# Small transfers of a decoder kernel issued from GpSimd's queue instead of SyncE's

## The chip, the cores and the metric

The kernel runs on one core of a Trainium2 chip. A core has TensorE (PE, matrix products), VectorE (DVE), ScalarE (ACT), GpSimd (POOL) and SyncE (SP). Each works through its own instructions in order, and semaphores tie them together. A DMA is issued by an instruction on one of these engines' queues, here SP's in the kernel before, and carried out by 16 DMA engines beside the others. The metric is the time of one execution on the device in microseconds.

## The reference

The kernel computes a trunk of two layers over 512 tokens of 1024 channels, in float32. Layer 0 mixes tokens by sliding-window attention, layer 1 by a gated delta rule; each is followed by a feed-forward product with a short convolution in its gate.

```
x += swa_sink_attention(rms_norm(x))        # 16 heads of 64, window of 128
x += (silu(causal_dwconv(gate) + b) * up) @ w_down
x += gated_deltanet(rms_norm(x))            # 8 key heads, 16 value heads of 128
x += (silu(causal_dwconv(gate) + b) * up) @ w_down
...
gc = cumsum(g);  decay = exp(gc_c - gc_s) below the diagonal
kk = k k^T;  a = 1 + strict_lower(beta * kk * decay)
u, w = solve(a, [v * beta, k * beta * exp(gc)])
v_new = u - w S;  o = q exp(gc) S + (q k^T * decay) v_new
S = S * exp(gc_last) + (k exp(gc_last - gc))^T v_new
```

The delta rule is a recurrence over blocks of tokens; within a block its triangular system `a` has to be inverted.

## The kernel before, in words

Activations are kept channel-major, 128 channels by 512 tokens in a tile. Every dense product runs over weight tiles of 128 by 1024 that the method `weight` (L125) loads to `raw` and splits in a high part `whi` (ACT, L134) and a low part `wlo` (DVE, L135); PE then makes three products per slice of 128 (L145 to L147), 24 matmuls for a tile. `raw`, `whi` and `wlo` have three buffers each, so that a new tile is loaded when the tile three back has been split.

The work that is not dense (attention, gates, decays, solve, recurrence) is written as generators. `pump` (L93) takes one step of whichever is due between two grains of the dense products. So the order of the instructions on every engine is fixed when the program is built; a scheduler of the framework then sets it and adds the semaphore waits. A DMA waits, besides its producers, for the one that used the same semaphore lane, eight DMAs earlier on its issuer's kind of queue (the names DMAHW0 to DMAHW7 and DMASW0 to DMASW7 in the orders below).

In the gated-delta layer much data takes a way through DRAM because its layout has to change between partitions:
- `decays` (L769) goes over eight head pairs `hk`. Rows of cumulated decays are broadcast to all partitions (`D<-rowd`, L796, two loads per pair); DVE subtracts and masks (L807), ACT takes the exponential (L809), and the result is stored (`Dd<-D`, L810). DVE then multiplies it into the products of keys (L815), and that goes to DRAM too (`kkd<-kd`, L817).
- `solve` (L822) reads the 32 by 32 triangles of all heads, with other partitions, in four loads (`X<-kkd`, L836), inverts them on DVE (L838 to L845), and stores them straight (`Td<-X`, L851, four) and transposed (`Nd<-t`, L859, six).
- `prologue` (L885) of each head pair loads `kk`, `D`, `kt` and `qd` (L897 to L900), then pieces of the inverses `NT` (L908, three) and `TT` (L911, four), and joins them to inverses of 128 rows by matmuls on PE (L920 on `NT`, L931 on `TT` and what follows). Two tiles are first set to zero by POOL (L895, L896). `vb` is loaded at L966 and `z` in `epilogue` at L1018. The values, `z` and the keys are stored at L694, L730 and L674.
- `run` (L1047) loads x and the constants, stores the residual `hd` (L1076) and writes the output (L1072); `h` comes back at L745.

All of this goes through `self.aux`, which is SP's queue (L79), or is written with `nc.sync` itself. SP issues the weights in the same queue, in program order.

Of the kernel before, what the change touches and what calls it, by code (L numbers as in the profile page):

```python
# [17 lines left out]
P = 128  # L18
# [6 lines left out]

# ---------------------------------------------------------------- host layout
def layout(x, positions, mixer_norm, ffn_norm, attn_w_in, attn_q_gain, attn_k_gain, attn_sinks,
           attn_w_out, gdn_w_in, gdn_conv, gdn_a_log, gdn_dt_bias, gdn_norm, gdn_w_out,
           ffn_w_up, ffn_conv, ffn_conv_b, ffn_w_down):
    """Arrays of the launch: the inputs in other orders, and constants of the shapes alone."""  # L30
    c = np.ascontiguousarray
    a = {}
    a["xT"] = c(x[0].T.reshape(KT, P, T))
    a["up"] = c(ffn_w_up.reshape(2, KT, P, 2, 24, P).transpose(0, 4, 3, 2, 1, 5)).reshape(2, 24, 2, P, 1024)
    a["down"] = c(ffn_w_down.reshape(2, 3, 8, P, 8, P).transpose(0, 1, 4, 3, 2, 5)).reshape(2, 3, 8, P, 1024)
    cols = []
    cols.append(mixer_norm.reshape(2, KT, P).transpose(2, 0, 1).reshape(P, 16))
    cols.append(ffn_norm.reshape(2, KT, P).transpose(2, 0, 1).reshape(P, 16))
    cols.append(ffn_conv.reshape(2, 3, 24, P).transpose(3, 0, 2, 1).reshape(P, 144))
    cols.append(gdn_conv[0].reshape(4, 32, P).transpose(2, 1, 0).reshape(P, 128))  # L40
    cols.append(gdn_norm[0].reshape(P, 1))
    cols.append(ffn_conv_b.reshape(2, 24, P).transpose(2, 0, 1).reshape(P, 48))
    w = attn_w_in[0]
    w = np.concatenate([w[:, 1024:1280], w[:, :512], w[:, 1280:], w[:, 512:1024]], axis=1)
    a["win"] = c(w.reshape(2, 4, P, 6, 256).transpose(3, 0, 2, 1, 4)).reshape(6, 2, P, 1024)
    wo = attn_w_out[0].reshape(2, 2, 4, 64, D).transpose(0, 2, 1, 3, 4).reshape(KT, P, KT, P)
    a["wout"] = c(wo.reshape(2, 4, P, KT, P).transpose(0, 3, 2, 1, 4)).reshape(2, KT, P, 512)
    a["rows"] = c(np.concatenate([attn_q_gain[0], attn_k_gain[0], attn_sinks[0]]))
    a["pos"] = c(positions[0].reshape(NB, P).T)
    a["freq"] = (500000.0 ** (-np.arange(0, 16, 2, dtype=np.float64) / 16)).astype(np.float32)  # L50
    i, j = np.arange(P)[:, None], np.arange(2 * P)[None]
    a["band"] = np.where((i + P - j >= 0) & (i + P - j < P), 0.0, -1e30).astype(np.float32)
    a["cols"] = c(np.concatenate(cols, axis=1))
    w = gdn_w_in[0].reshape(KT, P, -1).transpose(1, 0, 2)
    a["gin"] = c(w[:, :, :6144].reshape(P, KT, 48, P).transpose(2, 0, 1, 3)).reshape(48, P, 1024)
    a["gba"] = c(w[:, :, 6144:]).reshape(P, KT * 32)
    a["gout"] = c(gdn_w_out[0].reshape(2, 8, P, KT, P).transpose(0, 3, 2, 1, 4)).reshape(2, KT, P, 1024)
    a["grow"] = c(np.concatenate([gdn_a_log[0], gdn_dt_bias[0]]))
    a["tri"] = c(np.triu(np.ones((P, P), np.float32)))
    a["low"] = np.where(np.arange(P)[None] < np.arange(P)[:, None], -1e30, 0.0).astype(np.float32)  # L60
    a["ident"] = np.eye(P, dtype=np.float32)
    return a
# [5 lines left out]
class Builder:  # L68
    def __init__(self, tc, ctx, ins, out):
        self.tc, self.nc, self.ins, self.out = tc, tc.nc, ins, out  # L70
        pool = lambda name, bufs, **kw: ctx.enter_context(tc.tile_pool(name=name, bufs=bufs, **kw))
        self.const = pool("const", 1)
        self.wp = pool("wp", 3)
        self.big = pool("big", 36)
        self.tmp = pool("tmp", 8)
        self.small = pool("small", 3)
        self.gx = pool("gx", 1)
        self.ps = pool("ps", 8, space=bass.MemoryType.PSUM)
        self.aux = tc.nc.sync  # L79
        self.queue, self.now, self.seq = [], 0, 0  # L80
        self.dram = pool("dram", 1, space=bass.MemoryType.DRAM)
        nc = self.nc
        self.cols = self.const.tile([P, C_END], F32, name="cols")
        self.ident = self.const.tile([P, P], F32, name="ident")
        self.ones = self.const.tile([P, 1], F32, name="ones")
        nc.vector.memset(self.ones, 1.0)

    # ---- tasks that are traced between the grains of the dense products
    def spawn(self, gen, delay=0):
# [20 lines left out]

    # ---- allocation
    def psum(self):
# [10 lines left out]

    # ---- float32 operands as sums of two parts that one pass carries
    def weight(self, src, cols=1024, parts=1):  # L125
# [29 lines left out]

    # ---- 1/sqrt of a small tile, in place of x
    def rsqrt(self, y, x, n):
# [9 lines left out]

    # ---- rms norm: the operand (gain * h) in two parts, and 1/rms of each token
    def norm_tile(self, h, m, gain):
# [43 lines left out]
    def normalise(self, h, m, gain):  # L213
        """the operand again, with 1/rms in it"""
        nc = self.nc
# [7 lines left out]

    # ---- feed-forward
    def ffn(self, l, h, after):
# [32 lines left out]

    # ---- sine and cosine of the rotary angles, token-major
    def rope(self):  # L260
        nc = self.nc
# [3 lines left out]
        pos = self.ax.tile([P, NB], I32, name="pos", bufs=1)  # L265
        nc.sync.dma_start(pos, self.ins["pos"])
        fr = self.ax.tile([P, 8], F32, name="fr", bufs=1)
        nc.sync.dma_start(fr, self.ins["freq"].partition_broadcast(P))
        pf = self.ax.tile([P, NB], F32, name="pf", bufs=1)
# [62 lines left out]

    # ---- sliding-window attention
    def attn_setup(self):
        nc = self.nc
        rows = self.ax.tile([P, 144], F32, name="rows", bufs=1)
        nc.sync.dma_start(rows, self.ins["rows"].partition_broadcast(P))
        self.rows = rows
        self.gcol = self.ax.tile([P, 2], F32, name="gcol", bufs=1)
        nc.vector.memset(self.gcol, 1.0)  # L340
        for i in range(2):
            for j in range(2):
                nc.sync.dma_start(self.gcol[j * 64 + 16:j * 64 + 64, i:i + 1], self.ins["rows"][i * 64 + 16:i * 64 + 64].unsqueeze(1))
        nc.vector.tensor_scalar(self.gcol[:, 0:1], self.gcol[:, 0:1], 0.125, None, op0=ALU.mult)
        self.band = self.ax.tile([P, 2 * P], F32, name="band", bufs=1)
        nc.sync.dma_start(self.band, self.ins["band"])
        self.rope()

    def qk_norm(self, pss, dst, gain):
        """dst [P, 2, 8, 64], by pairs of blocks and (block, head) <- rotary(rms_norm(rstd * pss)),  # L350
        without the gain of the dims past the rotary ones"""
        nc = self.nc
# [188 lines left out]

    # ---- gated delta rule
    def in_tile(self, j, u):
# [5 lines left out]
    def conv(self, j, ps, dst, raw=False):  # L549
        """dst <- silu(causal conv of channels of tile j), channel-major"""  # L550
        nc = self.nc
# [10 lines left out]
    def turn(self, src):  # L562
        """[128, (4, 128)] psum <- four transposed blocks"""
        pt = self.psum()
# [8 lines left out]
    def gates(self, u, ready):  # L573
        """decays and beta of (token, block, head); gc and its exponential by rows too"""
        nc, gx = self.nc, self.gx
# [74 lines left out]
    def gdn(self, h, hd, stack, after):  # L650
# [87 lines left out]
        for half in range(2):  # L738
# [4 lines left out]
            for m in range(KT):  # L743
                if half == 0:
                    nc.sync.dma_start(hp[m], hd[m])  # L745
                hi, lo = self.weight(self.ins["gout"][half, m])
# [22 lines left out]
    def decays(self, sp, ready):  # L769
        """of each head: decay between two tokens of a block, and the strictly lower systems (rows by s)"""  # L770
        nc = self.nc
# [50 lines left out]
    def solve(self, sp, ready):  # L822
        """inverses of the 32-row triangles, two of each partition's (half, head, block)"""
        nc = self.nc
# [60 lines left out]
    def prologue(self, rx, hk, ready):  # L885
# [27 lines left out]
        jn = [(j, n) for j in range(2) for n in range(NB)]  # L913
        # 32 -> 64 rows
        px = self.psum()
# [21 lines left out]
        while "rq" not in ready:  # L937
            yield 1
        # products of queries and keys
        qk = self.psum()  # L940
# [6 lines left out]
        yield 2  # L947
        # 64 -> 128 rows
        px = self.psum()
# [97 lines left out]
    def run(self, stages):  # L1047
# [5 lines left out]
        for m in range(KT):  # L1053
            nc.sync.dma_start(h[m], self.ins["xT"][m])
            if m == 0:
                nc.sync.dma_start(self.cols, self.ins["cols"])
            if self.first and m in (0, 1):
# [3 lines left out]
            else:  # L1061
                self.norm_tile(h[m], m, gains[stages[0]])
        nc.sync.dma_start(self.ident, self.ins["ident"])
        if self.first:
# [3 lines left out]
        for i, s in enumerate(stages):  # L1068
# [4 lines left out]
            if s == "gdn":  # L1073
                hd = self.dram.tile([KT, P, T], F32, name="hd")
                for m in range(KT):
                    nc.sync.dma_start(hd[m], h[m])  # L1076
                h = self.gdn(h, hd, stack, after)
# [24 lines left out]
```

## Time and profile before

| | us |
|---|---|
| median of 3 runs | 1584.66 |
| fastest, slowest run | 1578.55, 1584.74 |
| span of the profiled execution | 1579.8 |
| PE busy | 1502.6 (95%) |
| DVE busy | 903.3 (57%) |
| ACT busy | 677.0 (43%) |
| POOL busy | 10.4 (1%) |

No time of the profiled execution is recorded beside its span; the span lies between the fastest run and the median. Busy times of engines overlap. The share of PE is a mean over the whole: the dense stages run at full PE and the gated-delta layer, roughly 640 to 1120 us, less so. A wait names the engine that stood still, the line it stood at, and what ended the wait. The landing of a DMA is the time from its issue on a queue to the end of its transfer.

### The profile page before, as it was taken

The numbers are of one execution on the slowest core, as the hardware profiler recorded it, in microseconds if no ns is written. First come the engines' busy times: TensorE is split into PE (matmuls) and PEld (weight loads), VectorE is DVE, ScalarE is ACT, GpSimd is POOL, SyncE is SP. The second block draws the span as 40 slices with busy tenths as digits, with TensorE's granted clock in tenths as the row PEclk, the third lists the DMA queues.
The fourth block names the chain that finished last, engine by engine and source line by source line (L and its number), as shares of the span: only waits on it lengthen the run. The fifth ranks groups of instructions, "written<-read, shape, count | busy, mean of one in ns | idle before, by whom it ended". The sixth has DMA issues, their size and how long they took to land. (4 is left out here: it accounts for less than half of the span.)

```text
span 1579.8 us, 20924 instructions
## 1 busy us (share of the span) xinstructions
PE 1502.6 (95%) x7914; PEld 1232.7 (78%) x7914; DVE 903.3 (57%) x1818; ACT 677.0 (43%) x1515; POOL 10.4 (1%) x21
## 2 busy tenths in 40 slices
PE   7999999999999999977888999989999999999998
PEld 7965688888888888766676887777788888888887
DVE  7675666445535658744478655555566644644652
ACT  6586643223323345534325456543453323322331
POOL 0000000000000000000000000000000000000000
PEclk9999999999999999998899999989999999999999
DMA  5201232332232243355685645544122232223222
GB/s 178 66 26 29 81 107 94 99 102 94 93 100 100 94 140 111 131 164 178 192 231 116 204 152 164 149 136 129 55 93 94 93 107 94 93 99 101 95 100 73
DMA packets 104572, 179.96 MB, mean 114 GB/s; under 512 B 45336, under 2 KB 57624, under 8 KB 104472
## 3 DMA queue, kind: packets, MB, share of 16 engines
q1 hardware_dynamic: 104472, 178.63, 35.8%
q8 instruction: 62, 1.02, 0.3%
q14 instruction: 38, 0.31, 0.1%
HBM read 153.60 MB, written 25.00 MB: 113 GB/s over the span
## 5 line engine op out<-in xcount | busy, mean ns | idle before, releaser
L147 PE MATMUL ps<-a,wlo 128*128 128x512 f32 x1736 | 685.7, 395 | 27.0 <-DVE wlo L135 27.0
L145 PE MATMUL ps<-a,whi 128*128 128x512 f32 x1736 | 695.0, 401 | 5.7 <-ACT whi L134 4.5
L146 PE MATMUL ps<-a,whi 128*128 128x512 f32 x1736 | 684.4, 394 | 0.0
L134 ACT CAST whi<-raw 128x1024 fp32r<-128x1024 f32 (+1 forms) x239 | 242.2, 1015 | 466.3 <-PE ps L146 394.5
L147 PEld LDWEIGHTS ps<-a,wlo 128*128 128x128 f32 x1736 | 329.6, 190 | 100.5 <-DVE wlo L135 30.2
L145 PEld LDWEIGHTS ps<-a,whi 128*128 128x128 f32 x1736 | 330.2, 190 | 79.9 <-ACT whi L134 5.4
L146 PEld LDWEIGHTS ps<-a,whi 128*128 128x128 f32 x1736 | 330.0, 190 | 66.8 <-DVE a L141 0.8
L135 DVE TENSOR_TENSOR wlo<-raw,whi 128x1024 fp32r<-128x1024 f32 (+1 forms) x239 | 280.3, 1174 | 61.7 <-ACT whi L134 58.3
L255 DVE TENSOR_TENSOR h<-h,ps 128x512 f32<-128x512 f32 x48 | 33.0, 688 | 148.5 <-PE ps L147 148.5
L240 DVE TENSOR_TENSOR t<-ps,rbc 128x512 f32<-128x512 f32 x48 | 33.2, 691 | 106.2 <-PE ps L147 106.1
L246 DVE TENSOR_TENSOR t<-ps,rbc 128x512 f32<-128x512 f32 x48 | 33.2, 692 | 90.8 <-PE ps L147 90.8
L244 ACT ACTIVATE t<-t 128x512 f32<-128x512 f32 x48 | 30.4, 632 | 97.7 <-DVE t L243 97.7
L145 PE MATMUL ps<-whi,a 128*128 128x256 f32 x192 | 57.2, 299 | 8.7 <-ACT a L189 8.7
L146 PE MATMUL ps<-wlo,a 128*128 128x256 f32 x192 | 55.5, 289 | 0.5 <-DVE wlo L135 0.5
L147 PE MATMUL ps<-whi,a 128*128 128x256 f32 x192 | 55.5, 289 | 0.0
L807 DVE SCALAR_TENSOR_TENSOR D<-D,both,low 128x128 f32<-128x128 f32 x64 | 18.1, 347 | 57.8 <-DMA D<-rowd 57.8
L145 PEld LDWEIGHTS ps<-whi,a 128*128 128x128 f32 x192 | 37.8, 197 | 10.7 <-ACT a L189 8.7
L559 DVE SCALAR_TENSOR_TENSOR t<-ps,cols,t 128x511 f32<-128x511 f32 (+2 forms) x48 | 35.6, 745 | 17.4 <-ACT t L557 10.9
L140 ACT CAST a<-t 128x512 fp32r<-128x512 f32 x48 | 30.0, 624 | 33.3 <-DVE t L247 33.3
L241 ACT ACTIVATE t<-t,cols 128x512 f32<-128x512 f32 x48 | 38.9, 811 | 2.0 <-DVE t L240 2.0
L146 PEld LDWEIGHTS ps<-wlo,a 128*128 128x128 f32 x192 | 37.9, 197 | 0.7 <-DVE wlo L135 0.7
L147 PEld LDWEIGHTS ps<-whi,a 128*128 128x128 f32 x192 | 37.8, 197 | 0.1
(245 smaller groups left out, 1431.3 us busy)
## 6 DMA issues: line engine op xcount, KB each, us to landing
raw<-in_up SPq DMA_DIRECT2D x96, 512.0 KB, 3.6
raw<-in_down SPq DMA_DIRECT2D x48, 512.0 KB, 3.6
raw<-in_gin SPq DMA_DIRECT2D x48, 512.0 KB, 4.7
raw<-in_gout SPq DMA_DIRECT2D x16, 512.0 KB, 3.7
raw<-in_win SPq DMA_DIRECT2D x10, 512.0 KB, 4.0
raw<-in_wout SPq DMA_DIRECT2D x16, 256.0 KB, 2.6
zd<-t SPq DMA_DIRECT2D x16, 256.0 KB, 4.8
D<-rowd SPq DMA_DIRECT2D x16, 256.0 KB, 12.7
```

Of the source, the lines that this page charges most:

```text
L134: nc.scalar.copy(hi[:, s], raw[:, s])
L135: nc.vector.tensor_tensor(lo[:, s], raw[:, s], hi[:, s].bitcast(F32), op=ALU.subtract)
L140: nc.scalar.copy(hi, src)
L145: mm(ps, w[0], x[0], start=first, stop=False)
L146: mm(ps, w[0], x[1], start=False, stop=False)
L147: mm(ps, w[1], x[0], start=False, stop=last)
L240: nc.vector.tensor_tensor(g, gu[0], self.bc, op=ALU.mult)
L241: nc.scalar.activation(y, g, AF.Identity, bias=self.col(C_FB + l * 24 + j), scale=self.col(cw + 2))
L244: nc.scalar.activation(y, y, AF.Silu)
L246: nc.vector.tensor_tensor(t, gu[1], self.bc, op=ALU.mult)
L255: nc.vector.tensor_tensor(h[m], h[m], ps, op=ALU.add)
L559: nc.vector.scalar_tensor_tensor(dst[:, i:], g[:, :T - i], self.col(cw + 3 - i), dst[:, i:], op0=ALU.mult, op1=ALU.add)
```

## The change

`self.aux` becomes GpSimd's queue, and the transfers that named SP's queue, except the weights (L133), the x tiles (L1054) and the output (L1072), go through `self.aux` too. Comments and some docstrings also go; no line number changes. The computation, the tiles and their buffers are the same.

```
-        self.aux = tc.nc.sync
+        self.aux = tc.nc.gpsimd
...
-        nc.sync.dma_start(pos, self.ins["pos"])
+        self.aux.dma_start(pos, self.ins["pos"])
...
-        nc.sync.dma_start(fr, self.ins["freq"].partition_broadcast(P))
+        self.aux.dma_start(fr, self.ins["freq"].partition_broadcast(P))
...
-        nc.sync.dma_start(rows, self.ins["rows"].partition_broadcast(P))
+        self.aux.dma_start(rows, self.ins["rows"].partition_broadcast(P))
...
-                nc.sync.dma_start(self.gcol[j * 64 + 16:j * 64 + 64, i:i + 1], self.ins["rows"][i * 64 + 16:i * 64 + 64].unsqueeze(1))
+                self.aux.dma_start(self.gcol[j * 64 + 16:j * 64 + 64, i:i + 1], self.ins["rows"][i * 64 + 16:i * 64 + 64].unsqueeze(1))
...
-        nc.sync.dma_start(self.band, self.ins["band"])
+        self.aux.dma_start(self.band, self.ins["band"])
...
-                    nc.sync.dma_start(hp[m], hd[m])
+                    self.aux.dma_start(hp[m], hd[m])
...
-                nc.sync.dma_start(self.cols, self.ins["cols"])
+                self.aux.dma_start(self.cols, self.ins["cols"])
...
-        nc.sync.dma_start(self.ident, self.ins["ident"])
+        self.aux.dma_start(self.ident, self.ins["ident"])
...
-                    nc.sync.dma_start(hd[m], h[m])
+                    self.aux.dma_start(hd[m], h[m])
```

In the order of instructions SP goes from 479 DMAs to 255, and POOL from none to 224. PE's order stays nearly the same. Three places show it. The first is SP's queue in the kernel before, at the decays of the first head pairs (D are the decay rows, Dd and kkd their stores in DRAM, zd a store of z, raw a weight tile):

```order
167 L133 DMA raw<-in_gin 128x1024 [waits DVE_49]
168 L810 DMA Dd<-D 128x1024 [waits DMAHW2_49,DMAHW1_49,Activation_49]
169 L817 DMA kkd<-kd 128x1024 [waits DVE_49]
170 L730 DMA zd<-t_5912 128x512 [waits DMAHW3_49,Activation_49]
171 L810 DMA Dd<-D 128x1024 [waits DMAHW4_49,Activation_49]
172 L796 DMA D<-rowd 128x4x128 [waits DMAHW5_49,DMAHW1_49]
173 L796 DMA D<-rowd 128x4x128 [waits DMAHW6_49]
174 L730 DMA zd<-t_5964 128x512 [waits DMAHW7_49,Activation_49]
175 L817 DMA kkd<-kd 128x1024 [waits DMAHW0_49,DVE_49]
176 L796 DMA D<-rowd 128x4x128 [waits DMAHW4_49]
177 L796 DMA D<-rowd 128x4x128 [waits DMAHW2_49]
```

The same place on POOL's queue in the kernel after:

```order
44 L810 DMA Dd<-D 128x1024 [waits DMASW1_49,DMASW0_49,Activation_49]
45 L817 DMA kkd<-kd 128x1024 [waits DVE_49]
46 L730 DMA zd<-t_5912 128x512 [waits DMASW2_49,Activation_49]
47 L796 DMA D<-rowd 128x4x128 [waits DMASW0_49]
48 L796 DMA D<-rowd 128x4x128
49 L810 DMA Dd<-D 128x1024 [waits DMASW5_49,Activation_49]
50 L730 DMA zd<-t_5964 128x512 [waits DMASW6_49,Activation_49]
51 L817 DMA kkd<-kd 128x1024 [waits DMASW7_49,DVE_49]
52 L796 DMA D<-rowd 128x4x128 [waits DMASW5_49]
53 L796 DMA D<-rowd 128x4x128 [waits DMASW1_49]
```

The weight loads that stood between the bounces are on SP's queue, where each waits for its buffer and its lane only. The bounces stand in nearly the same order among themselves; here the third pair's two D loads come ahead of the second pair's store Dd (row 49), where before that store stood ahead of them (row 171).

The second place is the end of the solve, on POOL in the kernel after (Nd and Td are the stores of the inverses, NT and TT the loads of the first head pair):

```order
100 L847 MEMSET X 128x2x32 [waits DVE_49]
101 L859 DMA Nd<-t_6895 64x16x32 [waits DMASW6_49,Activation_49]
102 L851 DMA Td<-X 64x32x32 [waits DMASW7_49,DVE_49,Pool_49]
103 L851 DMA Td<-X 64x32x32 [waits DMASW0_49]
104 L851 DMA Td<-X 64x32x32 [waits DMASW1_49]
105 L851 DMA Td<-X 64x32x32 [waits DMASW2_49]
106 L859 DMA Nd<-t_6895 64x16x32 [waits DMASW3_49]
107 L859 DMA Nd<-t_6899 64x16x32 [waits DMASW4_49,Activation_49]
108 L859 DMA Nd<-t_6899 64x16x32 [waits DMASW5_49]
109 L859 DMA Nd<-t_6903 64x16x32 [waits DMASW6_49,Activation_49]
110 L859 DMA Nd<-t_6906 64x16x32 [waits DMASW7_49,Activation_49]
111 L908 DMA NT<-Nd 32x8x32 [waits DMASW4_49,DMASW0_49]
```

On SP in the kernel before these DMAs stood in the same order, behind five weight loads in a row. They have all moved to POOL, where a MEMSET of X (L847) stands ahead of them.

The third place is the start, on DVE in the kernel after (a are the normalised inputs, h the x tiles, cols the gains):

```order
4 L344 TENSOR_SCALAR gcol<-gcol 128x1 [waits DMASW4_49,DMASW3_49,DVE_49]
5 L190 SCALAR_TENSOR_TENSOR a_105<-h_85,cols,a_104 128x512 [waits DMAHW0_49,DMASW0_49,Activation_49]
6 L135 TENSOR_TENSOR wlo<-raw,whi 128x512 [waits DMAHW1_49,Activation_49]
7 L135 TENSOR_TENSOR wlo<-raw,whi 128x512 [waits DMAHW2_49,Activation_49]
8 L190 SCALAR_TENSOR_TENSOR a_119<-h_86,cols,a_118 128x512 [waits DMAHW3_49,Activation_49]
9 L135 TENSOR_TENSOR wlo<-raw,whi 128x512 [waits DMAHW4_49,Activation_49]
10 L135 TENSOR_TENSOR wlo<-raw,whi 128x512 [waits DMAHW5_49,Activation_49]
11 L270 CAST pf<-pos 128x4 [waits DMASW0_49]
```

In the kernel before the first of these is a wlo of L135, and gcol (L344) and pos (L270) come behind all the L190. Now L344 stands ahead of them and waits for the loads of gcol on POOL's queue, and the first L190 waits for cols there.

## Rows read from the trace of the kernel before

**Rows 1.** The page: the span, and section 1, busy time by engine.
```profile
span 1579.8 us, 20924 instructions
...
PE 1502.6 (95%) x7914; PEld 1232.7 (78%) x7914; DVE 903.3 (57%) x1818; ACT 677.0 (43%) x1515; POOL 10.4 (1%) x21
...
```

**Rows 2.** Busy time by stretch; columns in the header row.
```profile
...
core 0: us, PE busy (x) PEld busy (x) DVE busy (x) ACT busy (x) POOL busy (x), PEclk, DMA share, GB/s
...
240.00:280.00 40.00, 40.00 (x179) 33.10 (x178) 23.19 (x29) 15.40 (x19) 0.00 (x0) 1.00 0.30 104
...
669.00:782.00 113.00, 85.76 (x360) 68.51 (x358) 50.58 (x119) 40.52 (x69) 1.19 (x2) 0.86 0.52 171
...
853.00:880.00 27.00, 20.90 (x169) 16.23 (x168) 17.10 (x37) 17.81 (x56) 0.00 (x0) 0.87 0.66 125
...
```

**Rows 3.** Waits of PE, 669 to 890 us: who waited for whom, total, times, longest.
```profile
...
PE ps L147 <- DVE wlo L135: 27.0, 7, 10.0
PE ps L567 <- ACT t L560: 6.0, 1, 6.0
...
```

**Rows 4.** Waits of DVE, 669 to 890 us.
```profile
...
DVE D L807 <- DMA D<-rowd: 57.8, 13, 11.7
...
DVE X L838 <- DMA X<-kkd: 2.4, 1, 2.4
...
```

**Rows 5.** The page, section 6: issues of D<-rowd, KB each, us to landing.
```profile
...
D<-rowd SPq DMA_DIRECT2D x16, 256.0 KB, 12.7
```

**Rows 6.** Waits of SP's DMA queue, 669 to 782 us.
```profile
...
SPq L133 <- DVE wlo L135: 17.3, 4, 6.9
SPq L817 <- DVE kd L815: 10.9, 6, 3.2
SPq L796 <- DMA Dd<-D: 8.5, 3, 5.7
SPq L810 <- DMA D<-rowd: 8.1, 2, 4.0
SPq L810 <- ACT D L809: 6.4, 3, 2.3
...
```

**Rows 7.** Line 133's weight loads, 669 to 782 us: landing.
```profile
...
DMA to landing us min/median/max: 6.7/14.0/16.5
```

**Rows 8.** Line 133's weight loads, 240 to 600 us: landing.
```profile
...
DMA to landing us min/median/max: 3.5/3.6/4.6
```

**Rows 9.** Line 851's issues: min/median/max ns of one.
```profile
...
L851 SPq DMA_DIRECT2D Td<-X x4: 635/1794/2417, 853.5 to 857.8; - x4
...
```

**Rows 10.** Line 911's loads TT<-Td: landing.
```profile
...
DMA to landing us min/median/max: 2.2/6.5/7.8
```

**Rows 11.** Line 836's loads X<-kkd: issue in ns, and landing.
```profile
...
L836 SPq DMA_DIRECT2D X<-kkd x4: 648/1696/2778, 783.8 to 788.7; - x4
...
DMA to landing us min/median/max: 6.0/6.1/6.3
```

**Rows 12.** Timeline of SP's queue, 850 to 882 us: start, length.
```profile
...
852.76 0.60 SPq L859 DMA_DIRECT2D Nd<-t  x1
853.46 6.78 SPq L851 DMA_DIRECT2D Td<-X  x4
...
865.57 1.58 SPq L908 DMA_DIRECT2D NT<-Nd  x2
...
```

**Rows 13.** Timeline of PE, 852 to 880 us.
```profile
...
871.43 0.24 PE L920 MATMUL ps<-NT,kk 32*32 32x32 f32 x2
...
874.49 0.22 PE L931 MATMUL ps<-TT,x 32*32 32x32 f32 x2
...
```

**Rows 14.** Timeline of SP's queue, 930 to 970 us: two kk loads.
```profile
...
934.95 0.32 SPq L897 DMA_DIRECT2D kk<-kkd  x1
...
968.16 0.32 SPq L897 DMA_DIRECT2D kk<-kkd  x1
...
```

**Rows 15.** Timeline of PE, 0 to 12 us: the first matmul.
```profile
...
8.68 0.58 PE L145 MATMUL ps<-whi,a 128*128 128x256 f32 x1 [8.68 <-ACT a L189]
...
```

## Prediction

> **What bounds the kernel now.** I read the page's shares first, then the busy time by stage, then the waits of PE, DVE and SP in the stages where PE is not full, then the landings of the DMAs that end those waits. PE is busy for 1502.6 of 1579.8 us [rows 1], so only 77 us can be won without less work on PE, while a stall of PE adds its full length. Outside the gated-delta layer PE has nothing to gain: from 240 to 280 us it is busy for 40.00 of 40 us [rows 2]. The same row gives the pace of dense work: 179 matmuls in 40 us are 0.223 us each, and a weight tile of 24 matmuls lasts 5.4 us. The idle time lies where small transfers through DRAM share SP's queue with the weights. From 669 to 782 us (the decays of eight head pairs) PE is idle for 27.2 us and its granted clock is 0.86; from 853 to 880 us (end of the solve) it is idle for 6.1 us [rows 2]. In the first stretch PE's wait is for wlo, the low half of a weight, 27.0 us in 7 waits up to the start of the recurrence [rows 3]. But DVE, which makes wlo, stands behind L807, the decay rows D<-rowd, for 57.8 us in 13 waits [rows 4]; one such load takes 12.7 us to land [rows 5]. A weight is late there because DVE is held in order behind a bounce through DRAM.
>
> **What the change removes: the weights leave that queue.** 224 of SP's 479 DMAs go to POOL; SP keeps weights, x and output. Between 669 and 782 us SP held its queue for 17.3 us for a weight buffer, and for 10.9 + 8.5 + 8.1 + 6.4 = 33.9 us for the bounce traffic's own producers [rows 6]. The first part no longer stands ahead of a bounce; the second goes to POOL with the bounces, whose order there is nearly the old one (the third pair's D loads gain one place on a store, which I leave out). Bounds: 0, if the transfers themselves are the limit, and -27.0 us, all of PE's wait. I take the weights' share of the holding: 27.0 x 17.3 / 51.2 = 9.1, so **-9 us**. The reverse shows as well: a weight takes 14.0 us to land in this stage [rows 7] against 3.6 in the feed-forward [rows 8], because it stands behind the broadcasts. That is worth nothing by itself, since PE's wait is DVE's wait for D, not for raw.
>
> The landing of 14.0 against 3.6 us says that much of the delay is inside the transfers and not at the issue [rows 7, 8]. The Trainium skill (DMA: Bandwidth & Descriptors, section "Issuing engines are not separate DMA queues") states that DMAs started by the scalar, sync or gpsimd engine run on the same 16 engines and interleave, and that starting them from several engines saves only the time to initiate them. By that rule the term would be nearer 0 than -9 and the forecast 9 us later.
>
> **What it adds: the price of a piece on POOL.** No DMA of before is issued by POOL, so its price is unknown; its trace has 21 POOL instructions [rows 1]. I count pieces, the runs of contiguous bytes that a transfer's shape has: 2048 in each Td<-X (64x32x32) and X<-kkd, 1024 in each Nd<-t, 256 in each NT and TT load (32x8x32), 512 in each D<-rowd, 128 in a plain tile. The lower end is SP's price: a Td<-X takes 1794 ns to issue [rows 9], or 0.9 ns per piece. The upper end is a small load's whole landing: 6.5 us for TT's 256 pieces [rows 10], 25 ns per piece (D<-rowd's 12.7 us for 512 gives the same [rows 5]). Below the lower end, an issue that costs nothing would still leave the landings. I take **3.0 ns**, from the nearest row with many pieces, X<-kkd, whose whole transfer lands in 6.1 us [rows 11].
>
> **Solve end.** This is where the price falls on PE. Today the first Nd store is issued at 852.76, Td takes SP 6.78 us, NT loads begin at 865.57 [rows 12]; PE's first L920 (needs NT) is at 871.43 and its first L931 (needs TT) at 874.49 [rows 13]. That is 21.7 us, and PE's instruction order puts only two dense tiles in it, so nothing is in hand: it already waits 6.0 us there, at L567 [rows 3]. After the change the same 17 DMAs go one by one through POOL: 6 x 1024 + 4 x 2048 + 3 x 256 + 4 x 256 = 16,128 pieces. At 3.0 ns these are 48.4 us; with the last landing at TT's minimum of 2.2 us [rows 10], since POOL spaces them out, 50.6. Minus 21.7: **+29 us**, all on PE. The ends are 0.9 ns: 14.5 + 2.2 - 21.7 = -5, and 25 ns: +384.
>
> A POOL DMA stands in no row here, so the rule that bears on it is told alone. The Trainium skill (Advanced Engine Details and Errata, section "DGE: Hardware vs Software") gives about 1 us to the first byte for descriptors made by GpSimd's cores and about 600 ns for the hardware's. An estimate by these figures alone is 17 x 0.4 = 6.8 us in place of the 29, which would bring the sum to about 0.
>
> **X load.** Four transfers of 2048 pieces. Now about 4 x 1.7 us of issue and 6.1 us of landing [rows 11], 12.9 us, of which DVE shows 2.4 us as a wait [rows 4]. After: 24.6 + 6.1 = 30.7, so 17.8 more. DVE stands at X in order, ahead of the next wlo; the three wlo buffers made before it hold 3 x 5.4 = 16.2 us of PE work [rows 2]. About 2 us are left, and I take **+3** for the first matmuls at the lower clock after a stall. Ends 0 (0.9 ns) and +182 (25 ns).
>
> **Decays and recurrence.** A head pair of the decays brings POOL two D<-rowd, one Dd, one kkd and two zd, 1536 pieces or 4.6 us at 3.0 ns, in a stage of 113 / 8 = 14.1 us [rows 2]: hidden. A head pair of the recurrence brings kk, D, kt, qd (768), three NT, four TT, vb, z and two vd, 3456 pieces or 10.4 us, in a period of 968.16 - 934.95 = 33.2 us [rows 14]: hidden. The waits that POOL's queue takes over: a Dd waits for ACT's exponential, with zd and the next D loads behind it and DVE's L807 waiting for these, as on SP; a MEMSET of TT or NT waits for PE's last use, with the next pair's loads behind it, and those write the same tiles and waited for it before. Both **0**; the cover is gone above 9.2 and 9.6 ns per piece.
>
> **Start.** cols, ident, rows and gcol stand ahead of DVE's first L190 and L135: 576 pieces, 1.7 us at 3.0 ns. PE starts at 8.68 us on the a of L189 [rows 15], and it would be late only if gcol landed after about 7. I take **0**, with +8 at 25 ns (14.4 us). The hd stores and h loads are 16 plain tiles with no PE work that needs them soon: 0.
>
> **Sum.** -9 + 29 + 3 + 0 + 0 = +23. From the profiled execution's span, 1579.8 + 23 = 1602.8 [rows 1]. The median of the runs, 1584.66, lies 4.9 above that span, so I carry the same 4.9: **1608 us**.
>
> **Rivals.** The price p of a piece decides among them. With the solve end at 16,128 p - 19.5 and the decays at -9, the sum is zero at 1.8 ns. About 0.5% is what can be told from no change, 8 us either way: faster below 1.3 ns, slower above 2.3 ns.
> - Faster: POOL issues about as SP does (0.9 ns), and the weights no longer stand ahead of the bounces. Solve end -5, decays -9: -14, 1571 us; with all of PE's 27.0 us in the decays, 1553. For it: 17.3 us of SP's holding are for weight buffers [rows 6], and PE's 27.0 us are the largest wait in that stretch [rows 3]. Against it: the loads' own landing of 12.7 us, which the change does not touch [rows 5].
> - No change: p between 1.3 and 2.3 ns, or a dearer DMA start in place of dearer pieces, so that the solve end's loss (+2 to +17) and the decays' gain (0 to -9) cancel: about 1585. For it: 17 transfers at SP's own 0.4 to 1.8 us sum to the present 15 us or so [rows 9, 12]. What the Trainium skill gives for the first byte (above) would lead here if it were the whole price.
> - Much slower: p = 8.7 ns, the geometric middle of 3.0 and 25. Solve end 140.3 + 2.2 - 21.7 = +121; X load 71.3 + 6.1 - 12.9 - 16.2 = +48; the decays then bring POOL 13.4 of 14.1 us, so that their gain is lost; the recurrence 30.1 of 33.2, just hidden. Together +169, 1754 us. For it: a single issuer in order for stores and loads with no slack behind. Against it: the 25 ns rows are landings in a shared queue, not issues.
>
> **How the numbers follow.** The forecast (2.3 to 5 ns) has a chance of 0.38, with 1593 to 1655 of its own: at 5 ns the solve end is +61 and the X load +18. Much slower, above 5 ns, 0.25. No change 0.15. Faster 0.22. So slower 0.63. The range reaches down to 1566, which takes in the likelier part of the faster case, and up to 1730, which is about p = 7.5 ns with the decays' gain lost; about 0.08 lies below and 0.12 above.
>
> **What would show it.** Right: the Td and Nd issues stretched over some 45 us on POOL's queue, and PE waiting at L920 or L931 for about 30 us on NT or TT, with full PE before and after; weights landing near 3.6 us in the decays; DVE's wait at L807 still the largest there. Wrong: a solve end of 22 us or less (POOL is as quick as SP), a wait at L807 much below 57.8 us (then the weights had held it up), or PE waits at every head pair of the recurrence on TT, D or qd (then POOL is the bound throughout). A start of PE well after 8.68 us would put a cost at the place where I put none.

## The result and the profile after

The changed kernel takes 1618.0 us (median of 4 runs, 1616.7 to 1621.3) against 1584.5 before; the ratio of the runs is 1.0221 [1.0201, 1.0242]. It is slower by 33.5 us; the profiled executions, on whose rows the terms below rest, differ by 39.7 us (1619.5 and 1579.8). The forecast was 1608, so the sign was right and the size near. But the terms that made the sum were not the ones measured, so the nearness is luck. The profile of the kernel after is of its slowest execution, so a few us of the lags below can be spread between executions.

The page of the kernel after (span, busy time by engine; section 3, the DMA queues: packets, MB, share of 16 engines):

```profile
span 1619.5 us, 20917 instructions
...
PE 1505.3 (93%) x7914; PEld 1235.6 (76%) x7914; DVE 903.2 (56%) x1818; ACT 677.3 (42%) x1515; POOL 145.9 (9%) x245
...
q1 hardware_dynamic: 36720, 123.88, 23.9%
q0 software_dynamic: 17552, 54.75, 14.4%
...
```

PE is nearly as busy as before (1505.3 against 1502.6 us [rows 1]); 37 of the 39.7 us are idle time of PE. POOL's 145.9 us are now mostly DMA issues, which its row counts. Where the idle time lies is seen by setting the same instruction of both kernels side by side. These are first or last starts from the view of a line's instructions:

| | before | after | lag |
|---|---|---|---|
| first L241 (feed-forward of layer 0) | 210.1 | 216.4 | +6.3 |
| first L807 (decays) | 677.2 | 684.2 | +7.0 |
| last L815 (decays) | 780.6 | 806.9 | +26.3 |
| first L838 (X has landed) | 793.7 | 824.0 | +30.3 |
| L847 (inversion done) | 851.3 | 876.9 | +25.6 |
| first L931 (first TT used) | 874.5 | 903.0 | +28.5 |
| last L958 (end of the last prologue) | 1109.5 | 1149.5 | +40.0 |
| end of the span | 1579.8 | 1619.5 | +39.7 |

So: start 7.0, decays 19.3, X load 4.0 and 4.7 given back behind it, solve end 2.9, recurrence 11.5. By stretch, PE's busy time (columns as in [rows 2]); the decays are the second row, now 132 us long:

```profile
...
core 0: us, PE busy (x) PEld busy (x) DVE busy (x) ACT busy (x) POOL busy (x), PEclk, DMA share, GB/s
0.00:40.00 40.00, 25.12 (x163) 24.63 (x164) 26.87 (x122) 21.82 (x63) 7.18 (x17) 0.91 0.55 173
675.00:807.00 132.00, 82.61 (x342) 66.43 (x342) 49.34 (x118) 39.39 (x66) 26.51 (x42) 0.81 0.72 142
...
878.00:903.00 25.00, 10.92 (x71) 8.36 (x71) 14.99 (x33) 16.50 (x54) 15.87 (x22) 0.79 0.77 157
...
```

In the first 40 us PE is busy for 25.1 us where it was 30.8 in the same view of before. In the decays it loses 49 of 132 us, against 27 of 113 [rows 2]. The waits of PE and of DVE from 669 to 890 us (who waited for whom: total, times, longest), PE's first:

```profile
...
PE ps L147 <- DVE wlo L135: 44.6, 5, 10.8
PE ps L567 <- ACT t L560: 10.8, 1, 10.8
...
```

The same view of DVE:

```profile
...
DVE D L807 <- DMA D<-rowd: 70.7, 12, 9.2
...
DVE X L838 <- DMA X<-kkd: 6.4, 2, 5.5
...
```

PE's wait for wlo grew from 27.0 to 44.6 us [rows 3], DVE's wait for the decay rows from 57.8 to 70.7 [rows 4], while a D<-rowd lands no later than before in the median: 12.5 us against 12.7 [rows 5]. A load that is no slower, and a longer wait for it: this points to loads that are issued later. The solve end, on POOL's timeline (start, length, instruction; in brackets the idle time before it and its releaser):

```profile
...
878.54 0.86 POOL L859 DMA_DIRECT2D Nd<-t  x1 [1.45 <-DVE tm L843]
879.39 4.36 POOL L851 DMA_DIRECT2D Td<-X  x4
883.75 4.08 POOL L859 DMA_DIRECT2D Nd<-t  x5
894.69 1.25 POOL L908 DMA_DIRECT2D NT<-Nd  x2 [6.86 <-DMA Nd<-t]
...
```

And on PE's timeline, the first use of NT and of TT:

```profile
...
897.49 0.24 PE L920 MATMUL ps<-NT,kk 32*32 32x32 f32 x2 [0.73 <-DMA NT<-Nd]
...
903.00 0.28 PE L931 MATMUL ps<-TT,x 32*32 32x32 f32 x2 [2.51 <-DMA TT<-Td]
...
```

The ten stores of 14,336 pieces are issued in 9.3 us; SP took 12.7 us from the first to the end of the last [rows 12]. Each Td<-X costs POOL 1.09 to 1.11 us; SP took 0.64 to 2.42, in the median 1.79 [rows 9]. From the first Nd to the first L931 it is 24.5 us against 21.7.

### The profile page after: what moved, and what is told of

It is laid out like the page before. It is cut to its first block, busy times and chain, and to the rows that moved or that the text cites. A ratio compares the mean times of both kernels' runs of the same rounds, so it can differ in the third digit from the quotient of the medians.

```text
span 1619.5 us, 20917 instructions
## 1 busy us (share of the span) xinstructions
PE 1505.3 (93%) x7914; PEld 1235.6 (76%) x7914; DVE 903.2 (56%) x1818; ACT 677.3 (42%) x1515; POOL 145.9 (9%) x245
## 3 DMA queue, kind: packets, MB, share of 16 engines
q0 software_dynamic: 17552, 54.75, 14.4%
## 4 chain that ended last, share of the span: by engine, by line
PE 76%; DMA 9%; DVE 6%; issue 4%; ACT 3%; POOL 2%; SPq 0%; POOLq 0%; ACTq 0%; DVEq 0%
PE ps L145 22%; PE ps L146 22%; PE ps L147 22%; DMA D<-rowd 3%; DMA Dd<-D 2%; DMA qd<-rowd 2%; PE ps L540 1%; DMA TT<-Td 1%; DVE wlo L135 1%; DVE a L559 1%; PE ps L505 1%; PE ps L567 1%; PE ps L943 1%; PE ps L530 1%; DVE tm L843 1%
## 5 line engine op out<-in xcount | busy, mean ns | idle before, releaser
L147 PE MATMUL ps<-a,wlo 128*128 128x512 f32 x1736 | 684.8, 394 | 44.6 <-DVE wlo L135 44.6
L146 PE MATMUL ps<-a,whi 128*128 128x512 f32 x1736 | 684.2, 394 | 0.0
L135 DVE TENSOR_TENSOR wlo<-raw,whi 128x1024 fp32r<-128x1024 f32 (+1 forms) x239 | 280.1, 1174 | 64.9 <-ACT whi L134 57.3
L240 DVE TENSOR_TENSOR t<-ps,rbc 128x512 f32<-128x512 f32 x48 | 33.2, 691 | 106.6 <-PE ps L147 106.4
L246 DVE TENSOR_TENSOR t<-ps,rbc 128x512 f32<-128x512 f32 x48 | 33.2, 692 | 90.8 <-PE ps L147 90.8
L145 PE MATMUL ps<-whi,a 128*128 128x256 f32 x192 | 57.8, 303 | 8.8 <-ACT whi L134 8.8
L807 DVE SCALAR_TENSOR_TENSOR D<-D,both,low 128x128 f32<-128x128 f32 x64 | 18.4, 346 | 78.0 <-DMA D<-rowd 70.7
L1076 POOL DMA_DIRECT2D hd<-h x8 | 4.3, 541 | 586.2 <-DVE h L255 586.2
L145 PEld LDWEIGHTS ps<-whi,a 128*128 128x128 f32 x192 | 38.6, 202 | 10.8 <-ACT whi L134 8.8
L241 ACT ACTIVATE t<-t,cols 128x512 f32<-128x512 f32 x48 | 38.9, 811 | 2.0 <-DVE t L240 2.0
## 6 DMA issues: line engine op xcount, KB each, us to landing
D<-rowd POOLq DMA_DIRECT2D x16, 256.0 KB, 12.5
```

Of the source, the lines that this page charges most:

```text
L135: nc.vector.tensor_tensor(lo[:, s], raw[:, s], hi[:, s].bitcast(F32), op=ALU.subtract)
L145: mm(ps, w[0], x[0], start=first, stop=False)
L146: mm(ps, w[0], x[1], start=False, stop=False)
L147: mm(ps, w[1], x[0], start=False, stop=last)
L240: nc.vector.tensor_tensor(g, gu[0], self.bc, op=ALU.mult)
L241: nc.scalar.activation(y, g, AF.Identity, bias=self.col(C_FB + l * 24 + j), scale=self.col(cw + 2))
```

## The experiments

Theory O (order): the issuing engine is part of what the framework's scheduler plans with, so the change also reorders instructions; the order is what costs. Theory F (ring): on POOL's queue stores land behind loads. Theory P (price) and Q (queue): POOL's queue itself is slower. All ratios are to the kernel before, run beside the kernel in question; its median lay between 1577.3 and 1584.5 us in these sets, so two kernels are compared by their ratios, and places within them by their profiled executions. The kernel after has 1.0221 [1.0201, 1.0242].

**The start.** `e1_start_on_sp`: the constants of the start by SP again, the rest of the change kept.

```
-        self.aux.dma_start(self.gcol[...], ...)   # cols, ident, rows, band, pos, fr likewise
+        self.nc.sync.dma_start(self.gcol[...], ...)
```

> The kernel after, with the constants of the start (cols, ident, rows, gcol, band, pos, fr) issued by SP again; all else stays on POOL. In the trace of after the first up-weight load comes 6.4 us later than in before (194.9 against 188.5), DVE waits 10.6 us at L344 for gcol ahead of its first L135. Theory: the start's 6.4 us are the four gcol loads and cols on POOL's queue (landing 7.6 and 6.2 us against 2.7 and 2.6) and L344's place ahead of the first wlo: 1618 - 6 = 1612, ratio to before about 1.018, first up-weight load near 188.5. Rival: what is late at the start is the weights and x on SP, or is given back before the decays: 1618, ratio 1.022.

1612.1 us, ratio 1.0186 [1.0165, 1.0207]: some 5 us less than after, with intervals that overlap a little. In its profile the start's lag is gone: the first L241 comes at 208.4 us (after 216.4, before 210.1). In the kernel after, DVE's first work stood behind a tiny load (view of DVE's timeline, 0 to 14 us):

```profile
...
11.67 0.15 DVE L344 TENSOR_SCALAR gcol<-gcol 128x1 f32<-128x1 f32 x1 [10.61 <-DMA gcol<-in_rows]
11.81 0.75 DVE L190 SCALAR_TENSOR_TENSOR a<-h,cols,a 128x512 fp32r<-128x512 f32 x1
12.48 1.29 DVE L135 TENSOR_TENSOR wlo<-raw,whi 128x512 fp32r<-128x512 f32 x2
...
```

L344 needs gcol, which lands 7.6 us after its issue, and stands ahead of the first wlo, which was at 6.77 us before. (In before gcol took 2.7 us, but was issued at 10.1 us and not at 3.0; cols, issued at the same moment in both, took 6.2 us on POOL and 2.6 on SP.) With the constants on SP, L344 is back at 21.6 us and does not wait. How much is the late landing and how much L344's new place was not separated.

**The decays: queue or order.** `e5_decays_on_sp` puts the loop's three transfers back on SP; `e2_dd_on_sp` only the store.

```
-            self.aux.dma_start(d["D"][hk], D)
+            self.nc.sync.dma_start(d["D"][hk], D)     # e2; e5 also D<-rowd and kkd
```

> The kernel after, with the three transfers of the decays' loop (D<-rowd, Dd, kkd) issued by SP again, among the weights; all else stays on POOL. If the decays' loss is in these three (theory F and rival P both say so), the lag against before falls from 30.3 us at the first L838 to some 8, total about 1597, ratio 1.008. If it comes from the weights' own queue colliding with the bounces, or from zd, bk and X on POOL, it stays near 1618.

1622.8 us, 1.0263 [1.0242, 1.0284]. Moving them back wins nothing: the stage from the first L807 to the last L815 is 126.8 us, after has 122.7, before 103.4. So a price of POOL's queue (P) on these three is not the cause.

> The kernel after, with only the decay stores (Dd<-D, L810) issued by SP again. Theory F (one ring in order): in after a Dd store is issued behind the next pair's D<-rowd on POOL's queue and lands only after them (12.9 us against 6.1), and the pair after that waits for its landing because there are two D buffers, so that the loads of two pairs never overlap; the stage from the first L807 to the last L815 took 122.7 us against 103.5. On SP's queue the store passes the loads: Dd landing 7 us or less, POOL's wait at L796 for Dd (26.6 us in 4) nearly gone, that stage about 105 us, total about 1603, ratio 1.012. Rival P (price): D<-rowd itself is dearer from POOL's queue (DMA share 0.73 against 0.52 in that stage), so the loads land as late as before and the total stays at 1618, ratio 1.022.

1620.9 us, 1.0238 [1.0203, 1.0273], the stage 122.7 us: theory F falls too. The second pair's Dd, now on SP's queue (landing in us, min/median/max of this one), is this; the same store on POOL in after stands below it:

```profile
...
DMA to landing us min/median/max: 15.6/15.6/15.6
```

And in after:

```profile
...
DMA to landing us min/median/max: 14.6/14.6/14.6
```

Both were issued within 2 us of the start of the third pair's D loads (695.5 in e2, 696.0 in after), just behind them, and both landed only with them. In these two rows it is the order of issue that puts a store behind loads, in one queue or in two; the third pair's store in e2, issued at 713.2 between the fourth pair's two loads, landed after 2.9 us. The Trainium skill (DMA: Bandwidth & Descriptors, section "Issuing engines are not separate DMA queues") states that DMAs started by these engines run on the same 16 DMA engines whichever engine started them. The two numbers agree with that: another queue was no way past the loads.

What the order does is seen on POOL's timeline in after, from the second pair's store on:

```profile
...
696.00 1.52 POOL L796 DMA_DIRECT2D D<-rowd  x2
697.84 0.56 POOL L810 DMA_DIRECT2D Dd<-D  x1 [0.32 <-ACT D L809]
...
712.72 1.51 POOL L796 DMA_DIRECT2D D<-rowd  x2 [12.38 <-DMA Dd<-D]
714.22 0.56 POOL L810 DMA_DIRECT2D Dd<-D  x1
...
```

The D loads of the third pair (696.00) are ahead of the second pair's Dd (697.84). This store lands with them, and the loads of the fourth pair need its buffer: 12.38 us idle, until 712.72. On SP in before the store went first (690.0), landed 6.2 us later, and the loads of the third and fourth pair went at 693.1 and 697.6 (rows 171 to 177 of SP's order, shown with the change). `e6_store_first` restores that one place, on POOL; `e7_loads_first` makes the exchange in the kernel before, on SP.

```
+            dd = self.aux.dma_start(d["D"][hk], D)
+            with self.tc.issue_after(dd.ins):        # e6, for hk == 1 only: issue order, no wait
                 nxt = rows(hk + 1)
```

> The kernel after, with one edge of issue order: the third pair's D loads are queued behind the second pair's Dd store on POOL, as they stood on SP in before; no queue changes, and no wait for the store's end. Theory O (order): what the decays lost is one overlap of two pairs' loads, because the Dd store was put behind loads that land 14 us later, and the pair after waits for that store; the kernels with the old order in time (before) load pairs at 693.1 and 697.6 us, after loads them at 696.0, 712.7. Then the stage falls from 122.7 to about 108 us and the total to about 1604 (ratio 1.013). Theory Q (queue): a second queue beside the weights' slows the bounces whatever their order (moving the three transfers back to SP's queue did not help, but their order stayed the new one there too): 1618, ratio 1.022.

1603.9 us, 1.0165 [1.0133, 1.0197]; the stage is 106.5 us, with the same queues as in after. POOL's timeline:

```profile
...
694.06 0.53 POOL L810 DMA_DIRECT2D Dd<-D  x1 [1.82 <-ACT D L809]
694.58 1.52 POOL L796 DMA_DIRECT2D D<-rowd  x2
...
698.60 1.51 POOL L796 DMA_DIRECT2D D<-rowd  x2 [1.40 <-DMA Dd<-D]
713.05 0.56 POOL L810 DMA_DIRECT2D Dd<-D  x1 [12.93 <-ACT D L809]
...
```

The fourth pair's loads (698.60) follow the third's by 4 us and wait 1.40 us for the store. One place in the order is 16 of the stage's 19 us. In the total less of it is sure: by the ratios e6 gains 0.6%, some 9 us, by the profiled spans 17.5.

> The kernel before, everything on SP, with one edge of issue order the other way: the second pair's Dd store is queued behind the third pair's D loads. Theory O: the loads of the third and fourth pair no longer overlap, one round of some 14 to 16 us more in the decays, total about 1598 (ratio 1.009). Theory Q: no POOL queue, no loss: 1583, ratio 1.000.

1586.7 us, 1.0064 [1.0039, 1.0088], the stage 110.3 us against 103.4: the sign of theory O without any POOL queue, at about half the size. The fourth pair's loads come 15 us behind the third's (705.1 and 690.3), but the fifth's follow by 10 (715.2), so that part is won back. The stage's 6.9 us alone would be weak evidence: it is 107.4 us in e4 and 105.9 in e11 below, which don't touch the loop.

`e3_d3_buffers` goes at the wait in another way: `name="D", bufs=3` in place of 2, so that a load needs the store of one pair earlier.

> The kernel after, with three buffers for D in the decays in place of two; nothing moves between queues. Theory F: the loads of a pair no longer wait for the store just ahead of them, two pairs' loads overlap, and the four loads of an overlap took 15.6 us at the stage's first pairs where two alone take 13 to 14; the stage falls from 122.7 to 100 us or less, total about 1598 (ratio 1.009) or below. Rival P: the transfers are the limit, D<-rowd's landing grows from 12.5 to 20 us and more, the stage stays near 120 us and the total at 1618.

1597.4 us, 1.0093 [1.0066, 1.0120]; the stage is 98.4 us. The first six loads, three pairs, in flight together:

```profile
...
L796 POOL DMA_DIRECT2D D<-rowd x6: 747/776/823, 673.8 to 678.9; - x6
...
DMA to landing us min/median/max: 8.7/12.3/13.1
```

Six land in no more time than two. POOL's wait at L796 for a Dd falls from 26.6 us in 4 to 12.3 in 1: a store behind loads still holds one pair back.

**The price of a piece.** `e4_solve_on_pool`: the kernel before, with X<-kkd, Td<-X and Nd<-t on POOL.

```
-                self.aux.dma_start(X[ms, i], ...)   # Td and Nd likewise
+                self.nc.gpsimd.dma_start(X[ms, i], ...)
```

> The kernel before, with only the many-piece transfers of the solve (X<-kkd, Td<-X, Nd<-t: 14 DMAs, 22,528 pieces) on POOL. The prediction's price of 3.0 ns per piece would give some 25 to 30 us more at the solve's end: about 1610 (ratio 1.017). The trace of after has POOL's issue of Td at 1.09 us and of Nd at 0.82 us, that is 0.27 to 0.5 ns per piece, and the solve's end 2.8 us longer: by that the total stays within 4 us, 1580 to 1587 (ratio 0.998 to 1.002).

1593.2 us, 1.0110 [1.0083, 1.0137], some 17 us: neither number. The issues are as short as in after (a Td<-X 1.10 us). The lag against before grows by 8.4 us at the X load and by 9.3 between the end of the inversion and the first L931. On SP's queue at the solve's end (timeline, 855 to 895 us):

```profile
...
864.35 4.66 SPq L911 DMA_DIRECT2D TT<-Td  x4
...
873.51 2.92 SPq L911 DMA_DIRECT2D TT<-Td  x2
...
877.22 0.82 SPq L911 DMA_DIRECT2D TT<-Td  x2
...
879.80 0.86 SPq L908 DMA_DIRECT2D NT<-Nd  x2
...
```

And SP's waits there, 856 to 885 us:

```profile
...
SPq L911 <- DMA Td<-X: 9.5, 2, 8.6
...
```

Eight TT loads now stand ahead of the first NT load, which in before was the first of them [rows 12], and SP is held for 9.5 us in two waits until a Td has landed; PE waits 7.3 us for NT, which it does not in before. So this run does not give the price alone; it shows again that a move reorders.

**The recurrence.** `e11_recur_on_pool`: the kernel before with only these loads on POOL (`self.nc.gpsimd` at L897 to L911, L966, L1018). `e8_recur_on_sp`: the kernel after with them, and the h loads, on SP. `e12_s_copy_first`: the kernel after with an edge on ACT.

> The kernel before, with only the loads of the recurrence (kk, D, kt, qd, NT, TT, vb, z) on POOL. In after the lag grows by 11.5 us from the first L931 to the last L958, with these loads on SP by 5.3 us. Theory: the loads on POOL and the order that follows from it (PE's L943 stands between the first two L931) cost 8 to 14 us by themselves: total about 1590 (ratio 1.007). Rival: the 11.5 us are the lower clock and the waits that follow from a late solve, none of it from these loads: 1.000.

1601.9 us, 1.0143 [1.0110, 1.0177], more than either. From the first L931 (880.8) to the last L958 (1130.2) the lag grows from 6.3 to 20.7 us: 14.4, with all else on SP. (The 6.3 arise ahead of it, where DVE gets X, still loaded by SP, 14.5 us later than in before and makes part of that up.)

The profiles of all runs say the same. From the first L931 to the last L958 it takes 233.3 to 235.5 us in the four kernels with these loads on SP (before, e4, e7, e9), 242.0 to 250.4 in the nine with them on POOL, and 240.2 in e8 below, which has them on SP and the stores on POOL. By stretch, in after:

```profile
...
903.00:1150.00 247.00, 222.35 (x1866) 187.94 (x1867) 132.08 (x309) 118.08 (x359) 69.17 (x120) 0.92 0.51 141
...
```

And in before:

```profile
...
875.00:1110.00 235.00, 216.64 (x1864) 185.03 (x1863) 132.60 (x311) 117.82 (x359) 7.88 (x13) 0.93 0.52 155
...
```

Of the 12 us more, 6.3 are idle time of PE and 5.7 a longer busy time for the same work, at a granted clock of 0.92 against 0.93.

> The kernel after, with the loads of the recurrence (kk, D, kt, qd, NT, TT, vb, z and h) issued by SP again among the weights; the stores stay on POOL. In after the lag against before grows from 28.5 us at the first L931 to 40.0 at the last L958. Theory: those 11.5 us come from the loads' later landing (TT, qd, z behind each other on POOL's queue, MEMSETs in it): lag constant from the first L931, total about 1607 (ratio 1.015). Rival: they come from the weights passing the loads, or from the changed order on ACT and DVE (PE's wait for ACT's S copy is 14.2 us against 3.4): no gain, 1618 (ratio 1.022), or a loss when SP's weight waits stand ahead of the loads.

1625.0 us, 1.0307 [1.0271, 1.0343]: a miss in the total. The lag grows by only some 5 us in the recurrence, but the first L931 comes at 915.0, 12 us later than in after. There too the eight TT loads stand ahead of NT on SP's queue, which is held for 8.9 us for Td, and PE waits 8.6 us for NT. The gain is lost ahead of the stage in which it arises.

```
+                with self.tc.issue_after(self.sc.ins):   # sc: the copy of the next pair's state, L1005
                     nc.scalar.activation(ob[j][:, s], o[j][:, s], AF.Copy, scale=...)
```

> The kernel after, with one kind of edge of issue order on ACT: the scaling of a pair's output (L1032, which waits through DVE for the qd load) is queued behind the next pair's copy of the state (L1005), in three pairs of which it stands ahead in after. No queue changes. Theory O: PE's waits at L983 for that copy (14.2 us in 3, against 3.4 in before) are what the order on ACT costs in the recurrence; they fall below 5 us, the lag's growth from the first L931 to the last L958 falls from 11.5 to about 4 us, total about 1610 (ratio 1.017). Theory Q: the loads themselves are late on POOL's queue (TT, qd, z), the wait moves to another instruction and the total stays at 1618 (ratio 1.022).

1618.4 us, 1.0226 [1.0190, 1.0262]. PE's waits in the recurrence, first in after:

```profile
...
PE ps L983 <- ACT S L1005: 14.2, 3, 5.7
...
PE ps L931 <- DMA TT<-Td: 4.8, 2, 2.5
PE ps L931 <- DVE x L924: 2.2, 1, 2.2
...
```

The kernel with the edge:

```profile
...
PE ps L931 <- DMA TT<-Td: 9.1, 3, 4.0
PE ps L931 <- DVE x L924: 8.2, 2, 5.3
...
PE ps L983 <- ACT t L1033: 3.6, 1, 3.6
...
```

The wait for the state's copy went, the waits for TT and for x took its place, and from the first L931 to the last L958 the lag grows by 14.5 us where theory O gave 4: here theory O fails. A wait for x of this length stands in before as well (view of before, 890 to 1160 us):

```profile
...
PE ps L931 <- DVE x L924: 9.6, 4, 3.4
...
```

The wait for TT does not. So the rows fit loads that come later on POOL's queue, as theory Q has it, but they do not show it. Which of its holds does it (in after POOL waits 67.9 us in 7 for PE ahead of the MEMSETs of NT, and 48.2 us in 5 for DVE ahead of the z loads, with the next loads behind) was not separated and stays open.

**Together, and a faster version.** `e10_after_start_d3` is the kernel after with the edits of e1 and e3. `e9_before_d3` is the kernel before with three D buffers.

> The kernel after with two edits together: the start's constants on SP, and three buffers for D. One alone gave -6 us and the other -20 us. If they are separate terms they add: 1618 - 26 = 1592, ratio 1.006, and what is left is the recurrence's 12 us or so. If the start's lateness is what the decays wait for, the sum is smaller than its parts: 1597 or more (ratio 1.009).

1591.1 us, 1.0073 [1.0049, 1.0097]: the interval holds both 1.006 and 1.009, so whether the terms add is not shown. In the profiles e10 is 2.9 us ahead of e3 at the first L807, and 6.5 us more come in the recurrence, where neither edit is.

> The kernel before, all on SP, with three buffers for D in the decays. With three buffers on POOL's queue the stage from the first L807 to the last L815 fell from 122.7 to 98.4 us; before's own is 103.4 and its PE waits 27.0 us there. Theory: overlap of two pairs' loads is worth one round here too: stage about 95 us, total 1572 to 1577 (ratio 0.994 to 0.997), a version faster than both. Rival: SP's queue is in order with the weights, whose waits for buffers (17.3 us) then stand ahead of the loads, and nothing is won: 1.000.

1564.3 us, 0.9904 [0.9873, 0.9936]: faster than both kernels, and by more than expected. Its stage is 95.6 us (before 103.4), and PE's wait for wlo from 669 to 890 us is 9.6 us where it was 27.0 [rows 3]; part of that comes back as a wait for whi, 12.3 us where it was 4.5:

```profile
...
PE ps L145 <- ACT whi L134: 12.3, 4, 9.0
...
PE ps L147 <- DVE wlo L135: 9.6, 4, 7.2
...
```

## Why the prediction was right in sign, and where it was wrong

- **Solve end, +29 us: wrong.** This was the term that made the sign. The price of 3.0 ns per piece was put on POOL's issue; measured, a DMA of 2048 pieces costs 1.09 us to issue, one of 128 (ktd<-t) 0.54, so (1094 - 540) / 1920 = 0.29 ns per piece, below the lower end of the bounds. The term was +2.9. The stores wait in transfer instead: an Nd lands after 9.6 us (median) where it took 3.3 before. The nearest row, a whole landing, was a poor stand-in for an issue; SP's own issue rows were nearer.
- **Decays, -9 us: wrong in sign.** The weights did leave the queue, and land after 10.3 us (median) in the stage instead of 14.0, but PE's wait grew. The prediction saw that the third pair's D loads had come ahead of a store and left it out, as a gain. It was the largest loss: the stage took 19.3 us more, of which e6 takes back 16. The error was to ask which instruction is issued earlier, and not which buffer's release now lies behind it.
- **X load, +3: +4.0 was measured,** and the inversion gave 4.7 back, for which no run was made. The size was right by luck: the term rested on 24.6 us of issue, and the four issues took 1.09 us each. What grew was the landing, 10.0 us (median) where it was 6.1 [rows 11]. No run here measures the part of the term that was for a lower clock after the stall.
- **Recurrence, 0: wrong, +11.5.** The cover of 10.4 in 33.2 us counted issue time; POOL is indeed free most of the period (busy for 69.17 of 247 us). That these loads on POOL make the loss is shown by e11 and by the length of this stage in all runs; it is in PE's idle time and in a longer busy time, about half each, which a sum of issue times doesn't show. What holds the loads stays open.
- **Start, 0: wrong, +7.0** (+6.3 at the first L241). The text said that PE would be late only if gcol landed after about 7 us. The wait for it ended at 11.6; a landing of 7.6 us on POOL was not priced.
- **Sum.** +23 was forecast and +39.7 (33.5 by the medians) measured. Two wrong terms, 26 us too high and 28 too low, nearly cancel, so the forecast came near by luck; start and recurrence make most of the rest. The rival "faster" had its condition met (a piece costs less than 0.9 ns) and still failed. None of the rivals had the order as its mechanism.

The first-byte rule cited in the prediction (Advanced Engine Details and Errata, section "DGE: Hardware vs Software", of the Trainium skill) gives about 1 us and 600 ns, so by an estimate from these two figures 0.4 us more per DMA. Of the eight ktd stores the quickest landed 2.3 us after its issue on POOL and 2.0 on SP, which is near it; the medians, 3.6 and 2.1 us, and cols, 6.2 and 2.6, are further apart than that.

## What to carry to other kernels

A move of transfers to another queue is also a change of the order in which they are issued, under a scheduler such as this one, whose orders changed with the queue: read the new order for each buffer that is stored and loaded again, and ask which release now stands behind a long load. If a wait is for a buffer, try one more buffer before another queue: it loosens the dependence on the order, and made both kernels faster here. Price an issue by an issue row, and a landing by a landing row.

## What the runs showed of the hardware

- Broadcast loads of 512 pieces of 512 bytes (D<-rowd) land in about the same time whether two, four or six are in flight: at most 14.4, 13.3 and 13.1 us in after (695 to 698 and 675 to 680 us) and in e3. Over the stage single ones took up to 17.6 us in after, with two in flight. So up to six they were a delay more than a rate, which is why overlap pays.
- A store issued just behind a pair of such loads landed with them, after 14.6 us on the same queue and 15.6 us on the other.
- POOL's issue time was steady for DMAs of 2048 pieces (1.09 to 1.11 us for Td<-X) where SP's was not (0.64 to 2.42, median 1.79), and longer for plain tiles (0.54 against 0.33 us).
- The DMA engines' busy share in the decays rose from 0.52 to 0.72 with fewer GB/s (171 to 142), also in e6 (0.71), where the stage was only 3 us longer than in before: the share didn't tell how long the stage took.
